# Small work given out per block of rows, six gate products moved, rotary halves by DMA, in a two-network kernel on one core

## The chip, the cores and the metric

The kernel runs on 1 core of one Trainium2 chip. The metric is the device time of one execution in microseconds; three runs were timed, and one more execution was profiled.

## The reference, cut to what matters

Two networks of two layers follow each other on 512 rows of width 1024, all in fp32. The second one, in which nearly all of the change lies, puts 16 meta rows in front (528 rows) and runs this mixer in each layer:

```python
proj = n @ w_in                      # q,k,v,z,a,b of branch A; q,k,v of branch B; index q, k, weights
o_a = gated_deltanet(aq, ak, av, az, aa, ab, ...)   # conv of 4, silu, l2 norms, chunked delta rule, norm * silu(z)
o_b = dsa_attention(bq, bk, bv, iq, ik, iw, ...)    # rotary, index scores, top 128 keys of each row, softmax
gates = sigmoid(n @ w_gate + b_gate)
y = gates[:, :, 0] * (o_a @ w_branch_a) + gates[:, :, 1] * (o_b @ w_branch_b)
h = h + y @ w_out                    # then a feed-forward part with a conv of 3
```

The delta rule solves a unit triangular system per block of rows and carries a 128x128 state for each of 4 heads. Rotary means x1*c - x2*s and x2*c + x1*s on the halves of a head. The index score of a row and key is the sum over 8 heads of relu(q.k) times a weight.

## The kernel before, in words

Data lies transposed: 128 features on the partitions, rows along the free side. Every dense product (`dense`, `products`) makes 128 output features at a time: for each of 8 blocks of 128 input features the weight's high and low halves (`whi`, `wlo`, both fp32r) meet the operand's halves in three matmuls, each in two column halves for 528 rows, so 48 matmuls a product, all on L145. The weight comes by one DMA on SyncE's queue into `wraw` (3 buffers), ScalarE casts the high half (L99), VectorE subtracts the low half (L100); both have 2 buffers. The result is evacuated from one of 2 PSUM buffers.

Work of the small kind (attention, selection, scores, preparation) stands as (cost, function) in the list `fill`. `product_done` runs, after the last matmul of a product, as many of them as the product's `budget` pays for, in an `issue_after` block: TensorE's instructions of that work queue behind that matmul. `soon` holds work for the next product's end, `pending` the steps of a norm, one per product. `flush` runs all of `fill`. The order on each queue is then set by the Tile scheduler from program order (priority) and readiness.

The mixer (`mixer_2`) has these stages. First four products for the index queries (`ev_iq`: copy, rotary, split into halves on 64 rows each), one 80-column product, one for the key of branch B, then four for its queries and one for its values with budget 4.5; `keys` turns the index keys, and 24 `scores` of a tile and head are in `fill`: one matmul of 128 rows (L880), one of 64 rows (L881), relu on ScalarE, one VectorE operation. `squares` (L764) sends one-column sums (L769) through `soon`; `kscale` and `decays` follow. Rotary (`rope`, L708) multiplies each swapped half into another place by VectorE, four pieces of 32 rows or two of 64, then two full operations.

Second, twelve products for q, k, v of branch A with budget 2 (`ev_a`: three convolution steps, tanh), with 3 x 17 `select` steps and 12 `attend` calls in `fill`. `select` takes 8 maxima at a time on VectorE (L999, L1001). `attend(k)` does the values of unit k-2 (L1067 on 16 rows of meta keys, L1070 on 128), the scores of unit k (L1027), the turning of unit k-1 (L1047, L1056). Then a flush.

Third, 20 products (four of z, sixteen of the gates, `ev_g` stores to DRAM on ScalarE's queue), each with one of 19 steps ahead of it: keys, `dn_prep` of each tile (L1164 to L1193), `dn_solve` (a forward substitution on VectorE, L1231 and L1233, with DMAs through DRAM on SyncE's queue), four small levels (`pair1` to `pair4`, L1255 to L1288) and the meta tile's `join1`, `join2`. Fourth, the recurrence over five tiles (`dn_read`, `dn_u`, `dn_write`, `dn_out`, `dn_store` with L1393). Fifth, 16 branch products (L1449) and the output product. The norms (`col_sums`, `diag`, `spread`) serve the whole kernel, as does `weight`.

## Time and profile before

| what | value |
|---|---|
| median of 3 runs | 2953.84 us (2943.05 to 2955.46) |
| profiled execution, its own time | 2948.39 us |
| its span | 2946.5 us |
| TensorE busy | 2849.4 us |
| VectorE busy | 1856.0 us |
| ScalarE busy | 1044.0 us |
| granted TensorE clock, mean over the span | 0.978 |

The span runs from the first to the last instruction. TensorE's matmuls are pipelined and their ends are modelled, so its busy time says that it had something in flight, not that it ran at its best: the pace is read from the starts of matmuls or from their count in a stretch. A clock of 1.00 is 2.4 GHz, 0.50 is 1.2 GHz. PEld is the loading of weights into the array, beside the matmuls.

### The profile page before, as it was taken

The numbers are of one execution on the slowest core, as the hardware profiler recorded it, in microseconds if no ns is written. First come the engines' busy times: TensorE is split into PE (matmuls) and PEld (weight loads), VectorE is DVE, ScalarE is ACT, GpSimd is POOL, SyncE is SP. The second block draws the span as 40 slices with busy tenths as digits, with TensorE's granted clock in tenths as the row PEclk, the third lists the DMA queues.
The fourth block names the chain that finished last, engine by engine and source line by source line (L and its number), as shares of the span: only waits on it lengthen the run. The fifth ranks groups of instructions, "written<-read, shape, count | busy, mean of one in ns | idle before, by whom it ended". The sixth has DMA issues, their size and how long they took to land.

```text
span 2946.5 us, 44576 instructions
## 1 busy us (share of the span) xinstructions
PE 2849.4 (97%) x18009; PEld 2505.8 (85%) x18009; DVE 1856.0 (63%) x3462; ACT 1044.0 (35%) x1939; POOL 14.1 (0%) x117
## 2 busy tenths in 40 slices
PE   7999999999999998998999999999999999999999
PEld 5767888877888887888998999999788998988897
DVE  7986535468653557699747564555788757565563
ACT  3444222345321233353633322223444633332222
POOL 0000000000000000000000000000000000000000
PEclk9999999999999999799999999999998999999999
DMA  4214333332333334121354232324221253432333
GB/s 123 65 33 121 93 100 94 100 93 72 99 94 96 98 97 116 45 68 51 109 132 148 86 93 80 101 85 123 58 58 51 82 146 111 116 92 85 104 89 91
DMA packets 509860, 272.23 MB, mean 92 GB/s; under 512 B 40112, under 2 KB 494918, under 8 KB 509398
## 3 DMA queue, kind: packets, MB, share of 16 engines
q1 hardware_dynamic: 493520, 245.24, 29.5%
q10 hardware_dynamic: 16134, 24.14, 2.5%
q8 instruction: 142, 2.33, 0.3%
q14 instruction: 64, 0.52, 0.1%
HBM read 249.11 MB, written 20.23 MB: 91 GB/s over the span
## 4 chain that ended last, share of the span: by engine, by line
PE 87%; DVE 8%; DMA 2%; ACT 1%; issue 1%; SPq 0%; ACTq 0%; DVEq 0%
PE mm L145 74%; PE mm L1449 2%; DVE wlo L100 1%; PE b L1070 1%; PE b L769 1%; PE a L398 1%; PE a L881 1%; DMA qkv<-xz 1%; DVE ac L708 1%; DMA ax<-gd 1%; PE c L423 1%; DVE m L999 1%; DVE ac L971 1%; PE b L1067 1%; PE a L1027 1%
## 5 line engine op out<-in xcount | busy, mean ns | idle before, releaser
L145 PE MATMUL mm<-xparts,whi 128*128 128x256 f32 (+1 forms) x6752 | 1428.5, 320 | 16.8 <-ACT whi L99 7.8
L145 PEld LDWEIGHTS mm<-xparts,whi 128*128 128x128 f32 x6752 | 1045.6, 191 | 115.6 <-issue 9.5
L99 ACT CAST whi<-wraw 128x1024 fp32r<-128x1024 f32 (+1 forms) x472 | 457.8, 970 | 1405.9 <-PE mm L145 1167.8
L145 PE MATMUL mm<-xparts,wlo 128*128 128x256 f32 (+3 forms) x3376 | 888.2, 320 | 11.6 <-DVE wlo L100 11.6
L100 DVE TENSOR_TENSOR wlo<-wraw,whi 128x1024 fp32r<-128x1024 f32 (+1 forms) x472 | 529.3, 1121 | 411.3 <-ACT whi L99 404.9
L145 PEld LDWEIGHTS mm<-xparts,wlo 128*128 128x128 f32 x3376 | 565.4, 191 | 61.8 <-DVE wlo L100 16.7
L145 PE MATMUL mm<-hh,whi 128*128 128x512 f32 (+2 forms) x1040 | 340.1, 354 | 0.0
L145 PE MATMUL mm<-hh,wlo 128*128 128x512 f32 (+2 forms) x1040 | 339.9, 354 | 0.0
L145 PE MATMUL mm<-hl,whi 128*128 128x512 f32 (+2 forms) x1040 | 339.1, 353 | 0.0
L145 PEld LDWEIGHTS mm<-hl,whi 128*128 128x128 f32 x1040 | 184.3, 188 | 27.5
L145 PEld LDWEIGHTS mm<-hh,wlo 128*128 128x128 f32 x1040 | 183.8, 188 | 27.9
L145 PEld LDWEIGHTS mm<-hh,whi 128*128 128x128 f32 x1040 | 184.0, 188 | 26.4
L1449 PE MATMUL mm<-xparts,whi 128*128 128x256 f32 (+2 forms) x512 | 87.6, 289 | 9.2 <-DVE ax L1463 5.0
L507 DVE TENSOR_TENSOR down<-mm,r 128x512 f32<-128x512 f32 x32 | 22.1, 692 | 106.8 <-PE mm L145 106.8
L366 DVE SCALAR_TENSOR_TENSOR val<-z,cw,val 128x512 f32<-128x512 f32 x120 | 84.8, 746 | 0.5
L1449 PEld LDWEIGHTS mm<-xparts,whi 128*128 128x128 f32 x512 | 71.9, 190 | 11.5 <-issue 5.7
L1501 DVE TENSOR_TENSOR fx<-mm,rbc 128x528 f32<-128x528 f32 (+1 forms) x44 | 30.7, 702 | 76.4 <-PE mm L145 76.4
L1514 DVE TENSOR_TENSOR fc<-fc,mm 128x528 f32<-128x528 f32 (+1 forms) x44 | 30.6, 696 | 73.4 <-PE mm L145 73.4
L1102 DVE TENSOR_TENSOR ac<-mm,rbc 128x528 f32<-128x528 f32 (+1 forms) x32 | 22.4, 699 | 77.7 <-PE mm L145 77.7
L145 PE MATMUL mm<-qkv,whi 128*128 128x256 f32 (+2 forms) x384 | 67.6, 284 | 0.0
L1506 DVE SCALAR_TENSOR_TENSOR fc<-fx,vcols,fc 128x528 f32<-128x528 f32 (+1 forms) x88 | 66.1, 757 | 1.4
L1508 ACT ACTIVATE fx<-fc 128x528 f32<-128x528 f32 (+1 forms) x44 | 28.1, 639 | 88.9 <-DVE fc L1506 88.8
(532 smaller groups left out, 3144.0 us busy)
## 6 DMA issues: line engine op xcount, KB each, us to landing
wraw<-in_w_up SPq DMA_DIRECT2D x152, 512.0 KB, 4.0
wraw<-in_w_down SPq DMA_DIRECT2D x96, 512.0 KB, 4.3
wraw<-in_w_in SPq DMA_DIRECT2D x52, 512.0 KB, 3.8
wraw<-in_w_gate SPq DMA_DIRECT2D x32, 512.0 KB, 4.2
wraw<-in_ab_w_in SPq DMA_DIRECT2D x20, 512.0 KB, 3.8
wraw<-in_c_w_in SPq DMA_DIRECT2D x16, 512.0 KB, 3.9
wraw<-in_w_out SPq DMA_DIRECT2D x16, 512.0 KB, 4.8
wraw<-in_w_down SPq DMA_DIRECT2D x32, 192.0 KB, 2.6
```

The source lines that it names most:

```text
L99: self.S.copy(hi[:, :n], raw[:, :n])
L100: self.V.tensor_tensor(lo[:, :n], raw[:, :n], hi[:, :n].bitcast(F32), op=ALU.subtract)
L145: ins = self.PE.matmul(o, lhsT=wt[:, k % chunk, :], rhs=xt[:, t0:t1], start=n == 0, stop=n == 3 * kb - 1)
L366: V.scalar_tensor_tensor(cacc[b], z[b][:, j:j + S], w, cacc[b], op0=ALU.mult, op1=ALU.add)
L398: PE.matmul(ps[:, :W], lhsT=qk[p][r0:r0 + 64, P * i:P * i + P], rhs=qk[4 + p][r0:r0 + 64, :W], start=True, stop=True)
L423: PE.matmul(po[:, 64 * j:64 * j + 64], lhsT=pts[:, P * c:P * c + P], rhs=vt[c][:, h:h + 64], start=c == 0, stop=c == i)
L708: self.V.tensor_tensor(t[o], raw[i], tab[1][i], op=ALU.mult)
L769: PE.matmul(p5[:n, i:i + 1], lhsT=q[:, t0:t0 + n], rhs=self.ones[:, 0:1], start=True, stop=True)
L1449: PE.matmul(o, lhsT=wt[:, k, :], rhs=xt[:, m0 + t0:m0 + t1], start=k == 0 and j == 0, stop=k == 3 and j == 2)
L1501: V.tensor_tensor(x[:, 2:2 + TG], ps, self.rbc, op=ALU.mult)
L1506: V.scalar_tensor_tensor(c, x[:, d + j:TG + j], w(j), c, op0=ALU.mult, op1=ALU.add)
L1514: V.tensor_tensor(c, c, ps, op=ALU.mult)
```

## The change

`fill` is now served after every block of 128 input features, with a credit of budget/8 a block (the overdraft carried on), each function queued behind that block's last matmul. The casts of a weight get a priority 150 instructions earlier. Matmuls on 16, 64 or other part rows get full rows where zeros or unused results allow it; sums over the meta tile use 128 rows. Rotary halves are moved by DMA on ScalarE's queue and multiplied in one operation (the table's sign is turned). The first stage's order is: two index products, the 80-column one, two index products, then key, queries, values with budget 4.8, the scores at cost 1. Six gate products come after every second one of the twelve projections, all with budget 4. `attend` is split into its parts, `dn_prep` into four. z is one tile and holds the output norm's gain; the decays' row term goes into the exponent's bias. The third stage has 14 products at a rate of 19/14 x 1.05 steps each. In a norm's `pending` for the turn between the networks an empty step is added.

```diff
+AHEAD = 150
 def weight(self, ap, kb, cols):
-        self.S.copy(hi[:, :n], raw[:, :n])
-        self.V.tensor_tensor(lo[:, :n], raw[:, :n], hi[:, :n].bitcast(F32), op=ALU.subtract)
+        with self.tc.high_priority(AHEAD):
+            self.S.copy(hi[:, :n], raw[:, :n])
+            self.V.tensor_tensor(lo[:, :n], raw[:, :n], hi[:, :n].bitcast(F32), op=ALU.subtract)
...
                     n += 1
+                self.run_fill(ins, budget / kb)
...
-    def run_fill(self, budget):
-        while self.fill and budget > 0:
+    def run_fill(self, ins, budget):
+        self.credit = min(self.credit + budget, budget)
+        while self.fill and self.credit > 0:
             cost, step = self.fill.pop(0)
-            budget -= cost
-            step()
+            self.credit -= cost
+            with self.tc.issue_after(ins.ins):
+                step()
...
     def col_sums(self, acc, T, scale, bias):
-            self.PE.matmul(ps[:n, i:i + 1], lhsT=acc[:, t0:t0 + n], rhs=self.ones[:, 0:1], start=True, stop=True)
+            self.PE.matmul(ps[:, i:i + 1], lhsT=acc[:, t0:t0 + P], rhs=self.ones[:, 0:1], start=True, stop=True)
...
     def rope(self, raw, tab, out, pool, h=64):
-            self.V.tensor_tensor(t[o], raw[i], tab[1][i], op=ALU.mult)
+            self.nc.scalar.dma_start(t[o], raw[i])
+        self.V.tensor_tensor(t, t, tab[1], op=ALU.mult)
         self.V.tensor_tensor(raw, raw, tab[0], op=ALU.mult)
         self.V.tensor_tensor(out, raw, t, op=ALU.add)
...
-            self.dense(w_in[:, 2824:3336], self.xparts, T2, ev_iq, early=True, lag=4)
+            self.dense(w_in[:, 2824:3080], self.xparts, T2, ev_iq, early=True, lag=4)
...
-            self.dense(w_in[:, 2568:2696], self.xparts, T2, ev_qk("k_norm", 4, [kT]))
+            self.dense(w_in[:, 3080:3336], self.xparts, T2, ev_iq, first=2, early=True)
...
-                self.split(ps, *ikT)
-            self.fill.append((99, lambda: None))
-            self.fill.append((0.5, keys))
+                S_.copy(ikT[0], ps)
+                for i in range(2):
+                    o = slice(64 * i, 64 * i + 64)
+                    V.tensor_tensor(ikT[1 + i][o], ps[o], ikT[0][o].bitcast(F32), op=ALU.subtract)
+            BS_ = 4.8
+            self.fill.append((BS_, lambda: None))
+            self.fill.append((1, keys))
+            self.fill.append((2, lambda: None))
...
-                PE.matmul(ps[:, :W], lhsT=q[r0:r0 + 64], rhs=ikT[1][r0:r0 + 64, :W], start=False, stop=True)
-                t = self.t(wk, [P, T2], "sqq")[:, :512]
+                PE.matmul(ps[:, :W], lhsT=q, rhs=ikT[1 + h % 2][:, :W], start=False, stop=True)
+                t = self.t(self.sp, [P, T2], "sq")
...
-                    self.fill.append((0.25 + 0.14 * i, lambda i=i, h=h: scores(i, h)))
-            self.dense(w_in[:, 2056:2568], self.xparts, T2, ev_qk("q_norm", 0, qT), budget=4.5)
-            self.dense(w_in[:, 2696:2824], self.xparts, T2, ev_v, budget=4.5)
+                    self.fill.append((1, lambda i=i, h=h: scores(i, h)))
+            self.dense(w_in[:, 2568:2696], self.xparts, T2, ev_qk("k_norm", 4, [kT]), budget=BS_)
+            self.dense(w_in[:, 2056:2568], self.xparts, T2, ev_qk("q_norm", 0, qT), budget=BS_)
+            self.dense(w_in[:, 2696:2824], self.xparts, T2, ev_v, budget=BS_)
...
-                V.scalar_tensor_tensor(sz[b][:, m0:], t, 1.0, z, op0=ALU.add, op1=ALU.mult)
+                V.scalar_tensor_tensor(z, t, 1.0, z, op0=ALU.add, op1=ALU.mult)
+                S_.activation(sz[:, b, m0:], z, AF.Copy, scale=hg)
...
-                    PE.matmul(po[:, j, :], lhsT=vt[:META, 4, :], rhs=tm[:, :n], start=True, stop=W == META)
+                    PE.matmul(po[:, j, :], lhsT=vt[:META if W == META else P, 4, :], rhs=tm[:, :n], start=True, stop=W == META)
...
-            for b in (4, 5, 6, 7, 8, 9, 10, 11, 0, 1, 2, 3):
-                self.dense(col(w_in, b), self.xparts, T2, ev_a, first=b, budget=2)
+            G1 = 6
+            for n, b in enumerate((4, 5, 6, 7, 8, 9, 10, 11, 0, 1, 2, 3)):
+                self.dense(col(w_in, b), self.xparts, T2, ev_a, first=b, budget=4)
+                if n % 2:
+                    g = n // 2
+                    self.dense(col(wg, g), tail, TE, ev_g, first=g, budget=4)
...
-                    V.scalar_tensor_tensor(e[:n, h, :n], pg[:, h, :], gc[:n, i, h:h + 1], self.mneg[:n, :n],
-                                           op0=ALU.subtract, op1=ALU.add)
-                S_.activation(e[:n, :, :n], e[:n, :, :n], AF.Exp)
+                V.tensor_tensor(e[:n, :, :n], pg, self.mneg[:n, None, :n].to_broadcast([n, 4, n]), op=ALU.add)
+                for h in H4:
+                    S_.activation(e[:n, h, :n], e[:n, h, :n], AF.Exp, bias=ng[:n, i, h:h + 1])
+                yield
...
-                    V.scalar_tensor_tensor(t[:, h, m:n], pt[:, h, m:], hg, sz[h][:, t0 + m:t0 + n], op0=ALU.mult, op1=ALU.mult)
+                V.tensor_tensor(t[:, :, m:n], pt[:, :, m:], sz[:, :, t0 + m:t0 + n], op=ALU.mult)
...
-            steps += [[lambda t=t: dn_prep(*t)] for t in tiles[1:]]
-            steps.append([lambda: dn_prep(*tiles[0]), dn_solve])
+            steps += [[part(i)] * 4 for i in range(1, 5)]
+            steps.append([part(0)] * 4 + [dn_solve])
...
+            rate = len(steps) / len(prods) * 1.05
+            for fs in steps:
+                self.fill.extend((1 / len(fs), f) for f in fs)
```

## Rows read from the trace of the kernel before

**Rows 1.** the page, busy time of each engine, share of the span, instructions

```profile
PE 2849.4 (97%) x18009; PEld 2505.8 (85%) x18009; DVE 1856.0 (63%) x3462; ACT 1044.0 (35%) x1939; POOL 14.1 (0%) x117
```

**Rows 2.** table by stretch: length, PE, PEld, DVE, ACT, POOL busy, clock, DMA, GB/s

```profile
1725.00:1800.00 75.00, 75.00 (x621) 75.00 (x621) 42.78 (x57) 21.17 (x25) 0.59 (x6) 1.00 0.29 83
1137.40:1250.30 112.90, 105.35 (x611) 87.98 (x610) 80.95 (x181) 40.98 (x71) 1.63 (x8) 0.80 0.23 66
1250.30:1417.80 167.50, 156.34 (x1159) 144.48 (x1159) 145.18 (x335) 79.69 (x193) 1.15 (x12) 0.97 0.23 63
1417.80:1528.30 110.50, 108.44 (x1130) 104.45 (x1127) 67.33 (x195) 48.98 (x133) 0.00 (x0) 1.00 0.50 130
```

**Rows 3.** the same for L145 alone: length, PE, PEld, clock, DMA

```profile
1250.30:1417.80 167.50, 116.28 (x854) 107.41 (x854) 0.97 0.23 63
```

**Rows 4.** table by stretch, TensorE alone: length, busy (count), clock, DMA, GB/s

```profile
1209.70:1230.20 20.50, 20.50 (x70) 0.50 0.06 17
1233.60:1243.80 10.20, 10.20 (x32) 0.50 0.19 53
1346.20:1356.50 10.30, 7.58 (x32) 0.50 0.37 103
2117.70:2127.90 10.20, 10.20 (x33) 0.50 0.19 51
2138.10:2148.40 10.30, 10.30 (x30) 0.50 0.20 52
2250.80:2267.80 17.00, 13.53 (x49) 0.50 0.22 63
```

**Rows 5.** list of waits of TensorE, whole run: total us, times, longest

```profile
PE b L769 <- ACT sqq L764: 12.8, 6, 4.9
PE mm L145 <- DVE wlo L100: 11.6, 9, 3.3
...
PE mm L145 <- ACT whi L99: 7.8, 8, 2.6
```

**Rows 6.** timeline of TensorE among the scores of layer 0: start, us

```profile
1200.65 0.39 PE L145 MATMUL mm<-xparts,whi 128*128 128x256 f32 x1
1200.87 0.28 PE L880 MATMUL a<-ikT,iq 128*128 128x256 f32 x1
1201.08 0.38 PE L881 MATMUL a<-ikT,iq 64*128 64x256 f32 x1
1201.39 0.39 PE L145 MATMUL mm<-xparts,whi 128*128 128x272 f32 x1
```

**Rows 7.** timeline of TensorE in the attention of layer 0

```profile
1301.33 0.48 PE L1067 MATMUL b<-ptm,vt 16*128 16x128 f32 x2
...
1302.90 0.62 PE L1027 MATMUL a<-kT,qT 128*128 128x272 f32 x2
...
1411.65 1.03 PE L1056 MATMUL b<-ident,s 128*128 128x128 f32 x8
1412.44 0.37 PE L145 MATMUL mm<-xparts,wlo 128*128 128x272 f32 x1
```

**Rows 8.** single lines: L708 (ns min/median/max), L1393 in the groups by line

```profile
L708 DVE TENSOR_TENSOR ac<-ax,tabI x32: 696/700/705, 1141.6 to 2082.3; 32x528 f32<-32x528 f32 x32
L708 DVE TENSOR_TENSOR ac<-ax,tabA x20: 701/703/707, 1181.8 to 2149.1; 64x528 f32<-64x528 f32 x20
...
L1393 DVE SCALAR_TENSOR_TENSOR t<-b,hg,sz 128x128 f32<-128x128 f32 (+2 forms) x40 | 12.0, 322 | 0.5 <-PE b L1390 0.4
```

**Rows 9.** DMA issues: count, KB each, median us to landing

```profile
qkv<-md SPq DMA_DIRECT2D x8, 128.0 KB, 4.7
...
vrows<-in_mix_norm ACTq DMA_DIRECT2D x1, 8.0 KB, 1.8
```

**Rows 10.** timelines of VectorE and TensorE around the solve of layer 0

```profile
1439.77 0.60 DVE L1193 SCALAR_TENSOR_TENSOR dec<-b,dmj,dec 128x128 f32<-128x128 f32 x2
...
1494.08 0.22 PE L1255 MATMUL a<-qkv,dec 32*32 32x32 f32 x2 [0.72 <-DMA qkv<-xz]
```

More of the change, by code (lines that the diff above doesn't have):

```diff
@@ L40, in __init__ @@
         self.n = 0
+        self.credit = 0
         self.vec, self.ahead = {}, []
@@ L198, in flush @@
             f()
-        self.run_fill(math.inf)
+        while self.fill:
+            self.fill.pop(0)[1]()
+        self.credit = 0
     def need_r(self):
@@ L289, in spread @@
             n = T - S
-            self.PE.matmul(pm[:, :n], lhsT=self.ones[:n, :], rhs=dm, start=True, stop=True)
+            self.PE.matmul(pm[:, :n], lhsT=self.ones, rhs=dm, start=True, stop=True)
             self.S.copy(bc[:, :n], pm[:, :n])
@@ L698, in turn_end @@
         sums.first = bc.first = True
-        self.pending = [sums, bc, bc1] + [lambda k=k: final(k) for k in range(0, KB, 2)]
+        self.pending = [sums, bc, lambda: None, bc1] + [lambda k=k: final(k) for k in range(0, KB, 2)]
     def rope(self, raw, tab, out, pool, h=64):
@@ L768, in sums @@
                     for i, t0, n in tiles:
-                        PE.matmul(p5[:n, i:i + 1], lhsT=q[:, t0:t0 + n], rhs=self.ones[:, 0:1], start=True, stop=True)
-                    V.tensor_copy(out[:, :4], p5[:, :4])
-                    V.tensor_copy(out[:META, 4:5], p5[:META, 4:5])
+                        PE.matmul(p5[:, i:i + 1], lhsT=q[:, t0:t0 + P], rhs=self.ones[:, 0:1], start=True, stop=True)
+                    V.tensor_copy(out, p5[:, :5])
                 self.soon.append(sums)
@@ L1071, in att_values, with attend @@
                                       start=False, stop=c == i)
-                for j, h in enumerate(hs):
-                    S_.copy(ob[h][:, t0:t0 + n], po[:, j, :])
+                S_.copy(ob[h][:, t0:t0 + n], po[:, j, :])
             units = [{"t": t, "hs": (h, h + 1)} for t in tiles for h in (0, 2)]
-            def attend(k):
+            def attend(k, cost):
+                fs = []
+                if k < len(units):
+                    fs.append(lambda: att_scores(units[k]))
                 if k >= 2:
-                    att_values(units[k - 2])
-                if k < len(units):
-                    att_scores(units[k])
+                    fs += [lambda j=j: att_values(units[k - 2], j) for j in range(2)]
                 if 1 <= k <= len(units):
-                    att_turn(units[k - 1])
+                    fs.append(lambda: att_turn(units[k - 1]))
+                fill.extend((cost / len(fs), f) for f in fs)
             fill = self.fill
@@ L1403, in mixer_2 @@
             steps.append([lambda: dn_keys(*tiles[4]), dn_scales])
-            steps += [[lambda t=t: dn_prep(*t)] for t in tiles[1:]]
-            steps.append([lambda: dn_prep(*tiles[0]), dn_solve])
+            gens = [dn_prep(*t) for t in tiles]
+            part = lambda i: lambda: next(gens[i], None)
+            steps += [[part(i)] * 4 for i in range(1, 5)]
+            steps.append([part(0)] * 4 + [dn_solve])
             meta = [f for lev in range(1, 4) for f in (lambda lev=lev: join1(4, META, lev), lambda lev=lev: join2(4, META, lev))]
@@ L1412, in mixer_2 @@
             steps[-1] += meta
-            prods = [lambda b=b: self.dense(col(w_in, b), tail, TE, ev_z, first=b - 12, budget=1) for b in range(12, 16)]
-            prods += [lambda b=b: self.dense(col(wg, b), tail, TE, ev_g, first=b, budget=1) for b in range(16)]
-            for k, p in enumerate(prods):
-                if k < len(steps):
-                    self.fill.append((1, lambda k=k: [f() for f in steps[k]]))
-                p()
-            for fs in steps[len(prods):]:
-                for f in fs:
-                    f()
+            prods = [lambda b=b: self.dense(col(w_in, b), tail, TE, ev_z, first=b - 12, budget=rate) for b in range(12, 16)]
+            prods += [lambda b=b: self.dense(col(wg, b), tail, TE, ev_g, first=b, budget=rate) for b in range(G1, 16)]
+            rate = len(steps) / len(prods) * 1.05
+            for fs in steps:
+                self.fill.extend((1 / len(fs), f) for f in fs)
+            for p in prods:
+                p()
+            self.flush()
             oparts = self.operands(T2)
```

70 lines of the change are left out of this document (37 added, 33 removed).

## The prediction, made before the change was run

> **What bounds the kernel now.** I began with the busy line of the page: TensorE is busy 97% of the span [rows 1]. That share alone hides what matters, so next came the table by stretch, where a plain stretch of the second network's feed-forward part shows the price of a product: 621 matmuls in 75.00 us at clock 1.00, so 0.1208 us each, 5.80 us for a product of 48 [rows 2]. In the mixer of layer 0 (layer 1 repeats it) I call the stretch with the index projections and scores A (1137.4 to 1250.3), the delta rule's twelve projections with the selection and attention B (to 1417.8), and z and the gates with the preparation and the solve C (to 1528.3) [rows 2]. C has TensorE busy 108.44 of 110.50 us at full clock: nothing is to be won there but the work itself. B holds 854 product matmuls [rows 3], 103.2 us at 0.1208, in 167.5 us; VectorE is busy 145.18 us of it, almost as long. So B has two bounds close together. A has a clock of 0.80.
>
> The clock is where the busy share misleads. Read at 0.50 are 20.5 and 10.2 us among the scores of layer 0, and 10.2 and 10.3 us in layer 1; and 10.3 and 17.0 us at the end of the twelve projections [rows 4]. The last two lie beside the longest wait of the list, 4.9 us for squares. The list of waits gives TensorE's idle: 12.8 us for the squares of L764 (both layers), 11.6 for the low halves of weights, 7.8 for their high halves [rows 5]. The reader is to see that the mixers lose by clumps, late weights and changes of the array's rows, and little by lack of work elsewhere.
>
> **The change part by part.** The sum is made against the profiled execution, 2948.39 us (span 2946.5 and 1.9 around it), which lies 5.45 us below the median of the runs shown, 2953.84.
>
> *Spreading the fill.* Scores go out one cost unit at a time after each 128-row block of a product (4.8 units a product, 0.6 a block) over six products instead of in clumps of 4.5 old units behind a product. If the clock then holds, the half-clock stretches of A (51.2 us in all) take half the time: gain 25.6 at most, 0 at least. I take 18, since the one-column sums stay clumped. Scores also wait for fewer buffers (a tile of their own).
>
> *Full rows.* Where the second matmul of a score runs on 64 rows, L145 to the next L145 takes 0.74 us for one product matmul and two score matmuls of 256 columns [rows 6]; three full-row matmuls at the product's price are 0.36, so 0.38 goes into the changes. 48 such pairs: 18.2 us. The attention values alternate 16 and 128 rows: eight records from 1301.33 to 1302.90, 1.57 us, against 0.79 for eight of full rows [rows 7], 0.78 for a unit of two heads; 16 units make 12.5. Together 30.7 at most; at least 0, if a switch between kinds of work costs the same at any number of rows. I take 20, nearer the high end, since the full-row rows sit between the same products. By the Trainium skill, page "TensorEngine Tiling (Array Packing)", section Key Properties, tiles of fewer rows operate independently and in parallel, while a change of mode drains the engine; the first half speaks against widening. By the first half alone the gain would be 0, by the second it would be the one taken; the rows above show no parallel gain.
>
> *Six gate products moved among the twelve projections, budget 4 each.* The fill of B (51 selection steps and 12 attention turns) costs 65 units in the code: 18 products at 4 hold 72, while 12 at 2 held 24 and the remaining 41 were flushed. The wait for the last squares was there because VectorE was behind with selection, convolution and weight halves at once; now a gate product stands between a projection and its sums. Gain: the 12.8 us of waits and half of the 7.58 and 13.53 busy at half clock there [rows 4], 10.6; I bound it by 0 and 23 and take 14, since VectorE stays loaded. VectorE bounds it: 145.18 us of work cannot shrink much, so B cannot come far below 150, which allows 17 a layer, more than is taken. With the products move their weight loads on SyncE's queue (in B only weights stand there, in C six fewer stand before the solve's transfers) and their stores on ScalarE's; both beside products, 0. The work of B on TensorE is not more than now: of the 854 matmuls, 17.8 products, almost six were already z and gates.
>
> *Weight halves issued 150 instructions earlier.* The two waits together are 19.4 us [rows 5], part of it at the very start. Bounds 0 and 19; I take 7. Nothing is removed; ScalarE and VectorE run the casts before evacuations that are due at the same time. A cast before an evacuation delays it by about a microsecond, and the next product of 5.80 us hides that.
>
> *Rotary halves by DMA.* 32 products of 32 rows at 0.700 us and 20 of 64 rows at 0.703 go from VectorE, 18 whole multiplications come [rows 8]: about 24 us less VectorE work. 52 transfers come, issued on ScalarE behind the copy of the same tile, and VectorE waits for them twice (product, and the tile overwritten in place). No row shows a transfer inside the chip; the nearest are a small load, 1.8 us, and a strided one, 4.7 us [rows 9]. 18 rotations make 32 to 85 us of latency, all beside products of 5.80 us with two buffers; on the path between 8 us gained (VectorE freed) and 25 lost. I take 2 lost, by the small load. By the Trainium skill, "DMA: Bandwidth & Descriptors", section "Anatomy of one DMA", a transfer has a fixed cost of some 2 us, so 18 would be 36 us; the two rows lie on both sides of it.
>
> *Small edits.* z as one tile: the 40 pieces of L1393 at 0.322 us [rows 8] become ten; each between 0.322 and four times that, 0 to 9 us of VectorE in the recurrence, take 3 on the path; the extra scaling on ScalarE lies beside C's products. Decays in the exponent's bias: four vector operations become one, one exponential four, beside the same products; 0, and at most a microsecond a tile if that cover fails. Removed memsets, one wider sum copy: 0.
>
> *What spreading costs.* Each clump breaks the stream for about 0.1 us (0.22 for the lone product matmul in [rows 6], not 0.12). Splitting attention and preparation makes some 50 more breaks in both layers: 0 to 12 lost, take 5.
>
> *The solve.* Its last input ends at 1440.37 and its first user runs at 1494.08: 53.7 us [rows 10]. After the change that input is made when 7 of 19 steps are spent, at 1.425 a product after 4.9 of 14 products; 9.1 are left, 52.8 us without the small work. This just covers it, and the eight first branch products stand behind. Taken as 0.
>
> Sum of gains: 18 + 20 + 14 + 7 + 3 - 2 - 5 = 55 us. Against the profiled execution that is 2893; as the median stands 5 higher, I forecast 2898.
>
> **The rivals.** *VectorE keeps B.* If VectorE's 145 us set the end of B, waits move from the squares to the evacuations, and the 14 are worth nothing, nor some 8 of the full rows (attention's part of the 20) and 6 of the weights: 2898 + 28 = 2926. For it: VectorE is busy 145.18 of 167.50 in B. Against: it idles at the end of B, where only attention is left.
>
> *The array does not care for rows:* the 20 go, 2918. Against it are the full-row rows; and it may join the first rival, giving about 2941. (It is what the independence that the Trainium skill's page "TensorEngine Tiling (Array Packing)" states would make of the change.)
>
> *The solve loses its cover.* Six products a layer stood behind the solve and no longer do: 12 x 5.80 = 70 us at the outside. The steps are paced by products, the solve's latency is not; it decides when the latency exceeds the 52.8 us by more than the branch products and small work take up, about 23 us, or when SyncE's queue, where its transfers and the weights share an order, holds weights back. With 70 lost and the gains left, 2898 + 70 = 2968; with the rotation's 25 as well, near 2990. For it: today's products already stop for that transfer (0.72 us before 1494.08). Against: today one step per product delays the later steps more than the latency does.
>
> *The spread does not hold the clock:* the half-clock stretches stay, 2898 + 18 = 2916.
>
> **How the numbers follow.** A measurement of this kernel can tell about 0.5%, 14.8 us, from no change: faster is below 2939, slower above 2969. My forecast (2875 to 2920, with the clock's rival inside) 0.55; VectorE keeps B 0.16; rows do not matter 0.07 alone and 0.09 joined with the former, about no change; the solve uncovered 0.07; all terms near their upper ends, about 2865, 0.06. Faster 0.80, same 0.11, slower 0.09 (four hundredths go from faster to the other two for what I have not seen). The range 2862 to 2950 reaches from the upper ends to just past the joined case.
>
> **What would show it.** Right: clock near 1.00 from the first score to the last; the sums after the scores without idle; score matmuls of 128 rows with 0.4 to 0.6 us from product to product; no wait near 5 us before the last squares; B's eighteen products in 150 us; waits for weight halves under 10 us in all. Wrong: VectorE above 95% in B with TensorE waiting for evacuations; L1255's successor waiting for the transfers of the solve with no products left; VectorE idle for the rotary transfers while a product's evacuation is queued behind; the clock at 0.50 among the scores again.

## The result, and the profile after

The changed kernel takes 2884.36 us (median of 4 runs, 2876.20 to 2886.91) against 2954.65 us for the kernel before, run beside it (2943.05 to 2959.70): a ratio of 0.9763, 95% interval 0.9728 to 0.9797. Against the profiled execution, where the sum of the prediction was made, it is 2884.84 us after and 2948.39 before, 63.6 us less; 55 were forecast. Time, sign and range came out as forecast. The shares of the terms did not, and the stages show it.

The busy line of the page, which answers to [rows 1], says next to nothing about it:

```profile
PE 2805.1 (97%) x18009; PEld 2496.6 (87%) x18009; DVE 1823.3 (63%) x3350; ACT 1056.0 (37%) x1977; POOL 15.7 (1%) x117
```

TensorE runs the same 18009 matmuls and is still busy 97% of the span. The change of the order let products wander between the stretches of [rows 2], so I cut each mixer at instructions in place of times: A from the norm's first sums to the decays' running sum, B to the last attention value, C to the first matmul of the recurrence. Here are A, B and C of layer 0, product matmuls alone (L145 before, L148 after), in the table by stretch: length, TensorE and weight-load busy with their counts, clock, DMA share, GB/s. First the kernel before:

```profile
1137.40:1263.40 126.00, 80.83 (x520) 74.10 (x518) 0.82 0.23 68
1263.40:1416.10 152.70, 104.27 (x761) 95.79 (x759) 0.97 0.21 59
1416.10:1528.30 112.20, 89.29 (x667) 82.84 (x667) 1.00 0.50 132
```

and the kernel after:

```profile
1138.90:1227.20 88.30, 65.21 (x489) 61.89 (x488) 1.00 0.45 123
1227.20:1371.20 144.00, 111.33 (x781) 101.13 (x779) 0.98 0.24 70
1371.20:1493.80 122.60, 95.70 (x678) 86.75 (x678) 0.95 0.45 114
```

A product matmul costs 0.1208 us [rows 2]. Take count times 0.1208 from the length, and what is left is what a stage pays beside its products. For A of layer 0: 126.0 - 520 x 0.1208 = 63.2 before and 88.3 - 489 x 0.1208 = 29.2 after. The remainder splits further: TensorE's idle (the gaps ahead of its instructions, summed), the loss to the clock (half of the time at 0.50), and the rest, which is small work and changes of rows. Both layers together, in us:

| stage | beside the products, before | after | idle | clock | small work and changes |
|---|---|---|---|---|---|
| A | 113.2 | 55.3 | 12.1 to 2.8 | 32.4 to 0.0 | 68.7 to 52.5 |
| B | 123.0 | 97.8 | 21.9 to 13.8 | 13.6 to 5.1 | 87.5 to 78.9 |
| C | 64.7 | 80.7 | 5.9 to 5.9 | 0.0 to 11.9 | 58.8 to 62.9 |

A gained 57.9 us, B 25.2, C lost 16.0. The sum is 67.1; 3.6 are given back elsewhere in the span (the spans differ by 63.5). The clock alone gave 29.0 of it (46.0 to 17.0); over the whole span it gave less, 18.7 (64.5 to 45.8), mainly since 10.3 us of loss now stand behind C, where 3.4 stood before.

The list of waits of TensorE, which answers to [rows 5] (total, times, longest). First one more line of the kernel before, for the solve's transfer, then the kernel after:

```profile
PE a L1255 <- DMA qkv<-xz: 3.8, 6, 1.4
```

```profile
PE mm L148 <- DVE ac L1126: 11.3, 4, 5.0
...
PE a L1283 <- DMA qkv<-xz: 4.9, 2, 2.8
...
PE mm L148 <- ACT whi L102: 3.1, 4, 1.5
```

The 12.8 us for the squares and the 11.6 for low halves are gone. In their place TensorE waits for L1126, the evacuation of a gate that now stands among the projections, 11.3 us in all. The solve's transfer was waited for before too, 3.8 us in six pieces of which [rows 10] shows one; now it is 4.9 in two, so the longest doubled and the total grew by 1.1.

Among the scores no time is at half clock any more. It has moved: in C and behind it stand 27.3 us in layer 0 (23.9 of them in one piece) and 17.1 in layer 1, where the kernel before had 3.4 us in each. The table by stretch, all engines (TensorE, weight loads, VectorE, ScalarE, GpSimd, clock, DMA, GB/s):

```profile
1484.10:1508.00 23.90, 23.90 (x131) 20.39 (x131) 8.90 (x19) 7.95 (x24) 0.00 (x0) 0.50 0.22 69
2361.30:2378.40 17.10, 17.10 (x119) 14.48 (x112) 4.82 (x10) 5.04 (x13) 0.00 (x0) 0.50 0.26 79
```

TensorE's timeline among the scores of layer 0, which answers to [rows 6], and in the attention, which answers to [rows 7]:

```profile
1199.66 0.40 PE L148 MATMUL mm<-xparts,wlo 128*128 128x256 f32 x2
1199.90 0.64 PE L148 MATMUL mm<-xparts,whi 128*128 128x256 f32 x4
1200.38 0.34 PE L893 MATMUL a<-ikT,iq 128*128 128x384 f32 x1
1200.56 0.34 PE L894 MATMUL a<-ikT,iq 128*128 128x384 f32 x1
1200.73 0.40 PE L148 MATMUL mm<-xparts,wlo 128*128 128x256 f32 x2
...
1336.50 0.47 PE L1090 MATMUL b<-ptm,vt 128*128 128x128 f32 x2
1336.81 0.83 PE L1093 MATMUL b<-ptr,vt 128*128 128x128 f32 x6
1337.40 0.37 PE L148 MATMUL mm<-xparts,wlo 128*128 128x272 f32 x1
```

A pair of scores of 384 columns takes 0.35 us from start to start of the product (1200.38 to 1200.73), as much as its 768 columns cost at a product's price (0.1208 us for 264 on average). Eight value matmuls take 0.90 us (1336.50 to 1337.40), where eight with 16 and 128 rows mixed took 1.57.

The rotary multiplications and their transfers, which answer to [rows 8, 9]: groups by line (busy, mean ns, idle ahead and its cause), then DMA issues (count, KB each, median us to landing):

```profile
L715 DVE TENSOR_TENSOR ac<-ac,tabA 128x528 f32<-128x528 f32 x10 | 7.1, 706 | 4.7 <-DMA ac<-ax 4.7
L715 DVE TENSOR_TENSOR ac<-ac,tabI 128x528 f32<-128x528 f32 x8 | 5.7, 707 | 2.7 <-DMA ac<-ax 2.7
L1420 DVE TENSOR_TENSOR t<-b,sz 128x512 f32<-128x512 f32 x8 | 5.5, 689 | 1.0 <-PE b L1418 0.7
```

```profile
ac<-ax ACTq DMA_DIRECT2D x20, 132.0 KB, 3.2
ac<-ax ACTq DMA_DIRECT2D x32, 66.0 KB, 2.5
```

The transfers land in 2.5 and 3.2 us, between the 1.8 and 4.7 from which their price was bounded, and VectorE waited 7.4 us for them in the whole run.

### The profile page after: what moved, and what is told of

The parts are those of the page before. It is cut to its first block, busy times and chain, and to the rows that moved or that the text cites. A ratio compares the mean times of both kernels' runs of the same rounds, so it can differ in the third digit from the quotient of the medians.

```text
span 2883.0 us, 44585 instructions
## 1 busy us (share of the span) xinstructions
PE 2805.1 (97%) x18009; PEld 2496.6 (87%) x18009; DVE 1823.3 (63%) x3350; ACT 1056.0 (37%) x1977; POOL 15.7 (1%) x117
## 4 chain that ended last, share of the span: by engine, by line
PE 85%; DVE 9%; DMA 2%; ACT 1%; issue 1%; ACTq 0%; SPq 0%; DVEq 0%
PE mm L148 73%; PE mm L1477 2%; DVE wlo L103 1%; DVE selw L1020 1%; DVE m L1018 1%; PE a L404 1%; DVE ac L986 1%; PE c L429 1%; DMA ax<-gd 1%; PE b L776 1%; PE a L1046 0%; DMA ac<-ax 0%; PE b L1093 0%; ACT whi L102 0%; DMA xz<-x 0%
## 5 line engine op out<-in xcount | busy, mean ns | idle before, releaser
L148 PE MATMUL mm<-xparts,whi 128*128 128x256 f32 (+1 forms) x6752 | 1426.5, 320 | 24.5 <-DVE ac L1126 11.3
L148 PEld LDWEIGHTS mm<-xparts,whi 128*128 128x128 f32 x6752 | 1042.1, 190 | 117.5 <-issue 14.9
L148 PE MATMUL mm<-xparts,wlo 128*128 128x256 f32 (+3 forms) x3376 | 882.2, 318 | 0.0
L148 PEld LDWEIGHTS mm<-xparts,wlo 128*128 128x128 f32 x3376 | 562.8, 190 | 44.4 <-DVE wlo L103 0.8
L148 PE MATMUL mm<-hh,whi 128*128 128x512 f32 (+2 forms) x1040 | 340.1, 354 | 0.0
L148 PE MATMUL mm<-hh,wlo 128*128 128x512 f32 (+2 forms) x1040 | 339.9, 354 | 0.0
L148 PE MATMUL mm<-hl,whi 128*128 128x512 f32 (+2 forms) x1040 | 339.1, 353 | 0.0
L148 PEld LDWEIGHTS mm<-hh,wlo 128*128 128x128 f32 x1040 | 183.8, 188 | 28.1
L148 PEld LDWEIGHTS mm<-hl,whi 128*128 128x128 f32 x1040 | 184.3, 188 | 27.4
L148 PEld LDWEIGHTS mm<-hh,whi 128*128 128x128 f32 x1040 | 184.0, 188 | 26.2
L1477 PE MATMUL mm<-xparts,whi 128*128 128x256 f32 (+2 forms) x512 | 90.9, 296 | 4.5 <-DVE ax L1492 4.4
L1477 PEld LDWEIGHTS mm<-xparts,whi 128*128 128x128 f32 x512 | 74.4, 196 | 7.3 <-issue 6.4
L1530 DVE TENSOR_TENSOR fx<-mm,rbc 128x528 f32<-128x528 f32 (+1 forms) x44 | 30.7, 702 | 76.4 <-PE mm L148 76.4
L148 PE MATMUL mm<-qkv,whi 128*128 128x256 f32 (+2 forms) x384 | 67.1, 283 | 3.5 <-DVE ax L1492 3.5
L148 PEld LDWEIGHTS mm<-qkv,whi 128*128 128x128 f32 x384 | 55.2, 188 | 3.9 <-ACT whi L102 3.9
```

Source lines behind the costliest of these rows:

```text
L148: ins = self.PE.matmul(o, lhsT=wt[:, k % chunk, :], rhs=xt[:, t0:t1], start=n == 0, stop=n == 3 * kb - 1)
L1477: PE.matmul(o, lhsT=wt[:, k, :], rhs=xt[:, m0 + t0:m0 + t1], start=k == 0 and j == 0, stop=k == 3 and j == 2)
L1530: V.tensor_tensor(x[:, 2:2 + TG], ps, self.rbc, op=ALU.mult)
```

## The experiments

Nine kernels take one part back or put one or two into the kernel before; three look for what is still lost. The figure to compare with is the changed kernel's 0.9763 (0.9728 to 0.9797). One per cent is 29.5 us.

| kernel | median us | ratio to before, 95% interval |
|---|---|---|
| narrow rows again | 2912.23 | 0.9853 (0.9837 to 0.9870) |
| before, full rows only | 2904.56 | 0.9841 (0.9824 to 0.9858) |
| clumps again | 2900.73 | 0.9816 (0.9791 to 0.9840) |
| casts not ahead | 2914.75 | 0.9858 (0.9834 to 0.9882) |
| before, casts ahead only | 2951.13 | 1.0000 (0.9982 to 1.0017) |
| before, full rows and casts ahead | 2912.38 | 0.9865 (0.9850 to 0.9879) |
| gates back | 2903.11 | 0.9821 (0.9805 to 0.9838) |
| gates back, with room | 2902.32 | 0.9834 (0.9818 to 0.9850) |
| rotary on VectorE | 2891.77 | 0.9786 (0.9772 to 0.9801) |
| solve earlier | 2886.35 | 0.9777 (0.9762 to 0.9791) |
| evacuations ahead | 2879.01 | 0.9750 (0.9725 to 0.9774) |
| evacuations ahead, four gates | 2882.84 | 0.9770 (0.9752 to 0.9788) |

**Rows, and what holds the clock.** Narrow rows back in the changed kernel, for the two kinds of matmul that the prediction priced (the sums and turns of the meta tile keep their full rows):

```diff
-                PE.matmul(ps[:, :W], lhsT=q, rhs=ikT[1 + h % 2][:, :W], start=False, stop=True)
+                r0 = 64 * (h % 2)
+                PE.matmul(ps[:, :W], lhsT=q[r0:r0 + 64], rhs=ikT[1 + h % 2][r0:r0 + 64, :W], start=False, stop=True)
...
-                    PE.matmul(po[:, j, :], lhsT=vt[:META if W == META else P, 4, :], rhs=tm[:, :n], start=True, stop=W == META)
+                    PE.matmul(po[:, j, :], lhsT=vt[:META, 4, :], rhs=tm[:META, :n], start=True, stop=W == META)
```

> The changed kernel with the second score matmul on 64 rows and the meta keys' values on 16 rows again, all else kept. Theory (a change of rows costs 0.38 us a score pair and 0.78 us an attention unit): TensorE is the bound in both stretches, so 18 + 12.5 = about 30 us come back, 2884 to about 2910, half in the scores, half in the attention, and the clock may fall to 0.50 among the scores again. Rival (spreading alone did it, the array does not care for rows): within 5 us of 2884, clock at full speed among the scores.

It cost 0.0090 of 2954.65, 27 us. TensorE's timeline of that kernel:

```profile
1199.80 0.34 PE L893 MATMUL a<-ikT,iq 128*128 128x384 f32 x1
1200.07 0.44 PE L895 MATMUL a<-ikT,iq 64*128 64x384 f32 x1
1200.44 0.39 PE L148 MATMUL mm<-xparts,wlo 128*128 128x272 f32 x1
1200.68 0.34 PE L893 MATMUL a<-ikT,iq 128*128 128x384 f32 x1
```

The same pair takes 0.64 us in place of 0.35, and the product behind it 0.24 (1200.44 to 1200.68) in place of 0.12: 0.41 a pair, beside the 0.38 taken from [rows 6]. Yet A's clock reads 1.00 with narrow rows too, so in this surrounding the rows are a direct price alone: small work rises by 18 us in A and 9 in B.

The other side, full rows alone in the kernel before:

```diff
-            ikT = [self.t(ip, [P, S], f"ikT{i}", F32R) for i in range(2)]
+            ikT = [self.t(ip, [P, S], f"ikT{i}", F32R) for i in range(3)]
+            for i in range(2):
+                G.memset(ikT[1 + i][64 - 64 * i:128 - 64 * i, :].bitcast(F32), 0.0)
...
-                PE.matmul(ps[:, :W], lhsT=q[r0:r0 + 64], rhs=ikT[1][r0:r0 + 64, :W], start=False, stop=True)
+                PE.matmul(ps[:, :W], lhsT=q, rhs=ikT[1 + h % 2][:, :W], start=False, stop=True)
...
-                    PE.matmul(po[:, j, :], lhsT=vt[:META, 4, :], rhs=tm[:, :n], start=True, stop=W == META)
+                    PE.matmul(po[:, j, :], lhsT=vt[:META if W == META else P, 4, :], rhs=tm[:, :n], start=True, stop=W == META)
```

> The kernel before with the full rows alone (second score matmul and attention's meta values on 128 rows with zeros, three tiles for the turned index keys). Theory (a change of the number of rows costs a fixed 0.38 us a score pair and 0.78 us a unit, wherever it stands): 25 to 31 us off the kernel before, 2925 to 2931. Rival 1 (in the kernel before the second part of a mixer hangs on VectorE, so that only the scores gain): 12 to 18 us, 2937 to 2943. Rival 2 (fewer stops also bring the clock back among the scores): 40 to 50 us, 2905 to 2915.

It gave 0.0159, 47 us: rival 2. A of both layers in its table by stretch:

```profile
1137.80:1246.60 108.80, 100.34 (x708) 92.03 (x707) 94.17 (x226) 45.99 (x79) 1.56 (x10) 0.91 0.27 79
2031.90:2131.00 99.10, 93.37 (x698) 86.92 (x697) 86.83 (x203) 45.09 (x78) 0.65 (x5) 0.98 0.24 65
```

The clock there was 0.82 (the first row of the tables above) and, in layer 1, 0.91 before:

```profile
2055.90:2168.70 112.80, 108.34 (x698) 92.22 (x697) 86.31 (x202) 45.25 (x78) 0.86 (x5) 0.91 0.21 57
```

In the split of above, 24 of the 48 us of span are small work and changes (12.5 in A, 11.6 in B) and 24 are clock (20.5 in A, 3.4 in B). So the full rows bring most of A's clock back by themselves (20.5 of 32.4 us), and they pay twice in the kernel before, once in the changed one.

The last of the three gives the budget out in one piece again:

```diff
-                self.run_fill(ins, budget / kb)
...
+                self.run_fill(ins, budget)
                 self.product_done(ins, lambda: evac(view), early)
```

> The changed kernel with one thing taken back: the whole budget of a product is given out behind its last matmul instead of an eighth behind each 128-row block. Theory (spreading the small work holds TensorE's clock): 30 to 50 us of half clock come back among the scores of the two layers and waits of a few us behind the clumps, so 2900 to 2912 us against about 2885. Rival (the clock is held by full rows, the new order of the first products and the early weight halves; the spread does nothing): scores at full clock, 2878 to 2890.

It cost 0.0053, 16 us by the medians, but the intervals just touch (0.9791 to 0.9840, 0.9728 to 0.9797), and one of its four runs took 2886.88 us. Half a miss for each: the time came out as the theory said, the place did not. A's clock stays at 1.00 and its lengths are the same (88.3 and 85.9 us against 88.3 and 85.3). The time is lost later. B of layer 0 ends with

```profile
1227.90:1369.20 141.30, 105.14 (x739) 96.40 (x737) 0.96 0.23 67
```

42 product matmuls less than after the change, and the list of waits has more for the gates' evacuation, 17.9 us in place of 11.3:

```profile
PE mm L148 <- DVE ac L1126: 17.9, 4, 4.8
```

In the split of above, both layers together, B pays 6.7 us more beside its products (idle and clock up, 6.0 and 5.1; small work down by 4.4) and C 11.1 (small work and changes up by 8.6, idle by 3.1). Beside full rows, spreading helps in B and C and does nothing for the clock among the scores. One thing this run does not take back: the code gives out 4.8 scores a product (cost 1 each), where the kernel before gave some seven to eleven (4.5 units at 0.39 to 0.67). So it shows that small clumps keep A at full clock in the new order, not that the old ones would. What holds the clock with narrow rows in the changed kernel, the spread or the fewer waits, was not separated.

**Weight casts.** The priority out of the changed kernel:

```diff
-        with self.tc.high_priority(AHEAD):
-            self.S.copy(hi[:, :n], raw[:, :n])
-            self.V.tensor_tensor(lo[:, :n], raw[:, :n], hi[:, :n].bitcast(F32), op=ALU.subtract)
+        self.S.copy(hi[:, :n], raw[:, :n])
+        self.V.tensor_tensor(lo[:, :n], raw[:, :n], hi[:, :n].bitcast(F32), op=ALU.subtract)
```

> The changed kernel without the priority of the weight casts. Theory (late weight halves were a wait of their own): TensorE's waits for L102 and L103 return, 7 to 12 us, 2884 to about 2893. Rival (the finer spreading already lets the casts through): within 3 us of 2884, waits for weight halves under 5 us in all.

It cost 0.0095, 28 us, far more than the 7 of the prediction and outside both forecasts of the run. Its list of waits:

```profile
PE mm L147 <- DVE wlo L102: 13.3, 10, 2.2
PE mm L147 <- ACT whi L101: 6.5, 6, 1.8
```

The waits themselves are as long as in the kernel before (19.8 us against 19.4), and half clock grows from 91.6 to 133.2 us, which is 21 more lost. The priority in the kernel before, alone:

```diff
-        self.S.copy(hi[:, :n], raw[:, :n])
-        self.V.tensor_tensor(lo[:, :n], raw[:, :n], hi[:, :n].bitcast(F32), op=ALU.subtract)
+        with self.tc.high_priority(150):
+            self.S.copy(hi[:, :n], raw[:, :n])
+            self.V.tensor_tensor(lo[:, :n], raw[:, :n], hi[:, :n].bitcast(F32), op=ALU.subtract)
```

> The kernel before with the weight casts' priority 150 instructions earlier alone. Theory (late weight halves cost what the list of waits shows, and the clock that falls behind them): the 19.4 us of waits go nearly all, and some of the half clock in the second part: 15 to 25 us, 2930 to 2940. Rival (the casts only come late where the small work is dense, as in the changed kernel; in the kernel before the price is the predicted 7 us or less): 2948 to 2956.

No gain. Its list of waits says why:

```profile
PE b L770 <- ACT sqq L765: 11.1, 4, 5.1
...
PE mm L146 <- DVE ax L967: 6.5, 2, 3.2
PE mm L815 <- DVE wlo L809: 6.2, 1, 6.2
```

The waits for `wlo` of `weight` are gone, and two new ones stand there: 6.5 us for an evacuation (L967) and 6.2 for the low half of the 80-column product (L809), which is cast outside `weight` and has no priority (1.0 before). Half clock rises from 129.1 to 153.9 us. VectorE's queue only handed the wait on. Rows and casts together in the kernel before (this diff and that of the full rows):

> The kernel before with the full rows and with the weight casts' priority, and nothing else. The rows alone gave 2905 us, the priority alone no change, while the changed kernel without the priority is 30 us slower. Theory (the priority pays once TensorE no longer loses its time to changes of rows): 2875 to 2893. Rival (it pays only with the spread and denser small work of the changed kernel): 2898 to 2912.

The rival: 2912, no better than the rows alone (intervals 0.9850 to 0.9879 and 0.9824 to 0.9858), with the 6.5 and 6.2 us of the run before still in its list. So the priority pays only with the other parts of the change. Which of them, was not separated. L967 and L809 wait for VectorE, so the rotary work taken off that engine suggests itself, but it is not enough: with that work back on VectorE and the priority kept (below), the changed kernel loses 7 us, not 28.

**The gates.** All sixteen gate products back behind the projections:

```diff
-            G1 = 6
+            G1 = 0
...
-                if n % 2:
+                if n % 2 and G1:
```

> The changed kernel with all sixteen gate products behind the attention again, twelve projections alone with budget 4 (48 of the fill's 65 units, the rest flushed), 19 steps over 20 products at a rate of 1.0. Theory (the attention's stretch is won by spreading, and the six products were lent to it by the solve, which gives 17 us back between attention and recurrence): the time from the attention's end to the recurrence loses its half-clock and waits there (8 us a layer shorter at equal products), while the flush costs about as much ahead of it; 2884 within 10. Rival (moving the products is what filled the end of the projections): 15 to 25 slower, with a wait of some 5 us for squares back.

It cost 0.0058, 17 us, as the rival said. Its list of waits:

```profile
PE mm L148 <- DVE ax L981: 14.9, 6, 4.8
PE mm L148 <- DVE wlo L103: 9.2, 2, 4.6
...
PE b L776 <- ACT sqq L771: 1.2, 2, 0.6
```

The rival's sign, a wait of some 5 us for the squares, did not come back (1.2 us in all, 12.8 in the kernel before): TensorE waits for an evacuation and for weight halves instead. So it was not the moved gates alone that removed that wait; no run that takes back a single part brings it back, and what removed it stays open.

The cost could have been want of room, as 12 products at 4 hold 48 of 65 units. So once more, with 5.5:

```diff
-                self.dense(col(w_in, b), self.xparts, T2, ev_a, first=b, budget=4)
+                self.dense(col(w_in, b), self.xparts, T2, ev_a, first=b, budget=5.5)
```

> The changed kernel with the six gate products back in the third part as in the run of before (gates back), but with a budget of 5.5 for the twelve projections, 66 units, so that the 65 units of selection and attention are given out beside them and nothing is left to flush. Theory (the moved gates are worth their room: 18 products at 4 hold the work, 12 at 4 did not): 2883 to 2892, no flush. Rival (VectorE needs a product's time without convolution between its steps; 12 products are too short for its work, whatever the budget): waits of TensorE for evacuations and weight halves of 15 us or more, 2898 to 2908.

The rival by its time: 2902, the same. Its mechanism did not show: the waits for evacuations of the mixers' products (L981, L1000) and for weight halves come to 14.2 us, against 14.4 in the changed kernel (L1126 and weight halves). What is new is a wait inside the attention, of the turning (L1068) for the scaled softmax weights on ScalarE:

```profile
PE b L1068 <- ACT s L1059: 9.2, 4, 3.7
```

B of layer 0 here, and in the kernel with evacuations ahead (below), which has the gates in place:

```profile
1225.10:1369.90 144.80, 130.45 (x953) 120.31 (x953) 124.30 (x283) 69.39 (x171) 1.00 (x10) 0.95 0.19 53
```

```profile
1227.60:1374.70 147.10, 143.52 (x1115) 135.88 (x1114) 131.91 (x291) 78.09 (x181) 1.00 (x10) 1.00 0.26 74
```

B takes 145 to 147 us with 953 matmuls or with 1115: gate products fill TensorE's holes in it nearly for nothing. That agrees with the bound of the prediction ("cannot come far below 150"), but that VectorE sets the length is argued, not shown: with the gates back it is busy 124.30 of 144.80 us and TensorE 130.45, and with the gates in place TensorE is busy 143.52 of 147.10. TensorE's idle in B of both layers is 29.3 us with the gates back and room, 13.8 in the changed kernel.

**Rotary halves** back on VectorE:

```diff
-            self.nc.scalar.dma_start(t[o], raw[i])
-        self.V.tensor_tensor(t, t, tab[1], op=ALU.mult)
+            self.V.tensor_tensor(t[o], raw[i], tab[1][i], op=ALU.mult)
...
```

> The changed kernel with the rotary halves multiplied piece by piece on VectorE again, no transfers. Theory (VectorE has room in the stretch of the scores, the transfers lie beside products): within 4 us of 2884, VectorE busy some 24 us more in the two mixers. Rival 1 (VectorE's relief counts): 8 or more slower. Rival 2 (the transfers' latency stands on the path): 5 or more faster.

It cost 0.0023, 7 us, and the intervals (0.9772 to 0.9801, 0.9728 to 0.9797) overlap: a small gain, not proved by the times, between the theory's 4 and the first rival's 8. The list of waits shows a wait of the projections for their evacuation on VectorE that the changed kernel has not:

```profile
PE mm L148 <- DVE ax L980: 11.4, 2, 6.0
```

But it stands in place of another: the gates' evacuation, 11.3 us in the changed kernel, is down to 0.2. By the split of above, 6.5 of the 11.6 us between the two profiled executions lie in A, where the rotations are (idle 2.8 to 6.3), and 3.1 in B.

**What C gave back.** Two kernels aimed at the losses. In the first, the solve goes out earlier:

```diff
-            rate = len(steps) / len(prods) * 1.05
+            rates = [2.7] * 3 + [0.95] * 8 + [1.6] * 3
```

> The changed kernel with one thing altered: the steps of the third part up to and with the solve are given out over its first three products (2.7 steps each), the seven steps of the meta tile over the next eight (0.95 each), the four levels behind the solve over the last three (1.6 each), in place of 1.425 a product throughout. Theory (the 17 us that the changed kernel gives back behind attention come from the solve's transfers returning when the products are used up, and from its small levels standing alone at half clock): the two waits of 2.1 and 2.8 us go, the half clock from the end of attention to the next norm falls from 44 us to under 20, 2866 to 2876 us. Rival 1 (the levels are as slow beside products; what is given back is the price of their many breaks): 2880 to 2888. Rival 2 (the preparation in three products makes VectorE and ScalarE late with evacuations and weight halves): 2888 to 2900.

Rival 1: 2886. The first level did run 8.7 us earlier in layer 0 (322.8 us after the mixer's start, 331.5 before), yet the recurrence began 3.2 later (358.1, 354.9), and the waits for the transfer stayed, at 5.1 us. In the second, the first operation of the evacuations goes ahead:

```diff
 def ev_g(b, ps):
-                V.tensor_tensor(g, ps, rtail(), op=ALU.mult)
+                with self.tc.high_priority(AHEAD):
+                    V.tensor_tensor(g, ps, rtail(), op=ALU.mult)
...
 def ev_a(b, ps):
-                V.tensor_tensor(x[:, 3:], ps, self.rbc, op=ALU.mult)
+                with self.tc.high_priority(AHEAD):
+                    V.tensor_tensor(x[:, 3:], ps, self.rbc, op=ALU.mult)
```

> The changed kernel with the first VectorE operation of the evacuations of the delta rule's projections and of the gates given a priority 150 instructions earlier, as the casts have. Theory (the new waits of 4.9 and 5.0 us for a gate's evacuation come from the order on VectorE, which takes selection steps first): these two waits go and with them 10 us of half clock, 2868 to 2878 us. Rival (VectorE's load sets the second part; the wait moves to the convolution, to a weight half or to attention): 2880 to 2888.

The waits for the gates' evacuation went as the theory said, from 11.3 us to 0.4, and B's clock is 1.00:

```profile
PE mm L148 <- ACT whi L102: 4.9, 5, 2.4
...
PE mm L148 <- DVE wlo L103: 3.0, 4, 1.3
...
PE mm L148 <- DVE ac L1128: 0.4, 1, 0.4
```

A part moved on, as the rival said: the waits for weight halves rise from 3.1 us to 7.9. The span fell by 8.3 us. The median, between the two forecasts, is 5 lower, which the intervals do not separate. It is the best kernel of the study, by a margin that is not proved. The last one adds to it four gates in B in place of six, and the rates:

```diff
-            G1 = 6
+            G1 = 4
...
-                if n % 2:
-                    g = n // 2
+                if n % 3 == 2:
+                    g = n // 3
...
-            rate = len(steps) / len(prods) * 1.05
+            rates = [2.7] * 3 + [0.8] * 9 + [0.9] * 4
```

> The changed kernel with evacuations ahead (as in the run of that name, 2879 us), four gate products among the twelve projections in place of six (after every third one, budget 4.3, 69 units), and in the third part, now of 16 products, the solve after three (2.7 steps each), the meta tile's seven steps over the next nine (0.8 each), the four levels at 0.9 a product. [...] Rival (the second part is as long with 16 products as with 18, VectorE setting it, so that two products a layer, 23 us in all, come to stand in the third part and eat the 20 us gained there): 2876 to 2890.

The rival by its time: 2883, where 2862 to 2874 had been hoped for. Half clock from the end of attention to the next norm fell from 44.4 us in the changed kernel (47.8 in the run with six gates) to 23.9, short of the hope of under 15, and the wait for the solve's transfer is still there, 6.5 us. Product matmuls beside the levels of layer 0, from the table by stretch of the products alone. The kernel after, then this one:

```profile
1470.00:1480.00 10.00, 8.16 (x50) 7.73 (x51) 0.83 1.06 261
1480.00:1490.00 10.00, 3.52 (x12) 1.99 (x11) 0.71 0.01 3
1490.00:1495.00 5.00, 0.59 (x1) 0.29 (x1) 0.50 0.00 0
```

```profile
1460.00:1470.00 10.00, 7.62 (x50) 6.22 (x49) 1.00 0.64 153
1470.00:1480.00 10.00, 7.67 (x55) 6.74 (x54) 1.00 0.30 98
1480.00:1490.00 10.00, 7.66 (x55) 6.81 (x55) 1.00 0.20 63
```

With products beside the levels the clock stays at 1.00; where they run out it reads 0.71 and 0.50. But in C of both layers, against the run with six gates, the clock returned 8.1 us, while small work and changes rose by 7.7 and idle by 5.8. Put among products, the levels cost more small work, changes and idle; put behind them, they run at half clock. Neither order was cheaper.

## Why the prediction was right

The time was right by a sum whose terms missed in both directions, so a part of the agreement is luck: the early casts and the rotation brought some 30 us more than their terms, C cost some 11 more than the 5 set aside for breaks and the solve, and the parts overlap.

- **Spreading, 18 us (0 to 25.6).** The effect came in full, the cause was wrong. All 51.2 us at half clock among the scores went, 25.6 us, and 6.8 more earlier in A. But "if the clock then holds" named the spread as what holds it; with full rows and the new order, small clumps hold it too, and full rows alone brought 20.5 us of A's clock in the kernel before. The step that failed is that the clock was given to one edit and the rows' price to another, as if the changes of rows were no part of why the clock fell. The spread's own worth, 16 us by medians whose intervals touch, lies in B and C.
- **Full rows, 20 (0 to 30.7).** Mis-sized: 27 in the changed kernel, near the upper bound from [rows 6, 7]; 47 where the clock still hung on it. The independence of small tiles that the Trainium skill states (page "TensorEngine Tiling (Array Packing)", section Key Properties) gives no gain here: the pair with 64 rows ran 0.41 us slower in this case's trace, which agrees with the same section's other half, that a change of mode drains the engine; the trace shows the cost, not the drain.
- **Six gates, 14 (0 to 23).** Right in place (B) and nearly in size: 17. The working was not: it counted the 12.8 us of waits for the squares as what the gates remove, and these waits do not return with the gates back (1.2 and 1.8 us); idle for evacuations, weight halves and the attention does. The bound held nearly, as B came to 144.0 us and 142.6, though that VectorE sets it is not shown.
- **Weight halves, 7 (0 to 19).** Mis-sized: 28 in the changed kernel, beyond the bound, since 21 of it is clock, which the bound from the waits left out; nothing in the kernel before, where the wait moved to L809 and an evacuation. That a term's price depends on the other parts is what the working left out.
- **Rotary, 2 lost (8 gained to 25 lost).** Wrong sign, small: 7 gained as it seems. The landing of 2.5 and 3.2 us was rightly bounded. (The fixed cost of some 2 us that the Trainium skill states, page "DMA: Bandwidth & Descriptors", section "Anatomy of one DMA", is given there for transfers that GpSimd issues; these were issued on ScalarE's queue and took a little more.) VectorE waited for it only 7.4 us in all.
- **Small edits, 3.** The 40 pieces of 12.0 us became ten (the eight full ones 5.5), but from the recurrence's first matmul to the next norm both layers together take 269.2 us against 268.4. In that stretch the loss to the clock grew by 6.9 us, from the half clock that moved there, while small work fell by 3.8 and idle by 2.2; so the 3 may be there, hidden, but no run takes the small edits back.
- **Breaks, 5 lost, and the solve, 0.** The solve's step failed. The 52.8 us of cover were worked out for the solve's return, and that was nearly right (waits of 2.1 and 2.8 us; 3.8 in all before). What the working did not ask is what stands beside the four levels after it: with 14 products for 20, hardly one was left, and C lost 11.9 us to the clock and 4 to small work and changes. This is the third rival's place at a quarter of its price.

The parts taken back one by one cost 27 (rows), 28 (casts), 16 (spread), 17 (gates) and 7 (rotary): 95 in all for a change of 70. They overlap; that waits and changes of rows feed the same half-clock stretches is the nearest reading, not shown part by part. Of the rivals, "VectorE keeps B" came in part: its waits moved to the evacuations, as it said, at 11.3 us, but the gates' gain stayed, and a priority for the evacuations took these waits away, so they came from VectorE's order. (The joined case, given as about 2941, is 2938 by its own terms; nothing hangs on it.)

## What to carry to other kernels

Price an edit in the surroundings in which it will stand: the rows gave 47 us in the old kernel and 27 in the new, the early casts 0 and 28, because idle, changes of rows and half clock are not separate accounts. Where a stretch has the clock at 0.50 with TensorE "busy" throughout, look at the changes of rows as well as at how few products stand there: full rows raised it in A, products beside the solve's levels kept it at 1.00 in C. Giving one kind of operation a higher priority on a loaded engine can move the wait to the next kind (in the kernel before TensorE's idle fell by no more than 1.6 us, 93.1 to 91.5; in the run with evacuations ahead a part moved), so read the list of waits again before counting a gain.

## What was not expected of the hardware

- The clock fell to 0.50 in stretches where TensorE's busy time is the whole stretch (23.90 of 23.90 us with 131 matmuls): the solve's levels and the first steps of the recurrence stood there, with no more than 25 matmuls of products (5 of L148, 20 of the branch products, L1477); and full rows alone raised A's mean clock from 0.82 to 0.91 and from 0.91 to 0.98.
- Getting a half-clock stretch back to full clock need not shorten the whole: in the last run half clock fell from 83.8 to 61.5 us against the run with six gates, and the span rose from 2874.7 to 2881.0.
- Transfers within the chip of 66 and 132 KB took 2.5 and 3.2 us from issue to landing, with 52 of them in the run: twice the bytes cost 0.7 us more.
